# A pair's scores moved forward, to stand behind the transposes of the last pair but one

## The chip, the cores and the metric

The kernel runs on one core of a Trainium2 chip. The core has a matmul engine (TensorE, in the profile PE, with its weight loads as PEld), three engines for elementwise work (VectorE = DVE, ScalarE = ACT, GpSimd = POOL), and SyncE (SP), which here issues most DMAs. PE writes to a small accumulation memory, PSUM, and the other engines carry the sums from there to the main on-chip memory, SBUF. Each engine works through its own list of instructions in a fixed order; between engines, semaphores hold an instruction back until what it reads has been written and what it overwrites has been read.

The metric is the device time of one execution in microseconds (us), the median of several runs. Lower is better.

## What is computed

One decoder layer over 256 tokens and 1024 features in float32: a token mixer (a convolution module beside a sparse attention with three branches), a cross-attention to 256 memory tokens, and a gated feed-forward. The change is inside the sparse attention, in its branches "slc" (selected blocks) and "win" (window). With 256 tokens the four blocks of 64 are all selected and the window of 512 holds all, so that both branches come to causal softmax attention of 16 heads over all earlier keys, each with keys and values of its own. Cut to that:

```python
def masked_softmax(s, mask):
    s = jnp.where(mask, s, -1e30)
    m = jnp.max(s, axis=-1, keepdims=True)
    p = jnp.where(mask, jnp.exp(s - m), 0.0)
    return p / jnp.maximum(jnp.sum(p, axis=-1, keepdims=True), 1e-30)

def win_block(args):                      # slc: the same with ks, vs
    ...
    bias = rel_bias[t5_bucket(dist)]...
    s = jnp.einsum("bqgrd,bkgd->bgrqk", qb, kb) * scale + bias
    p = masked_softmax(s, mask)
    return jnp.einsum("bgrqk,bkgd->bqgrd", p, vb)
...
o = g[:, :, 0] * o_cmp + g[:, :, 1] * o_slc + g[:, :, 2] * o_win
```

The other large matmuls that matter here are projections of the token mixer (`g_conv`, in the kernel "gc") and of the cross-attention's values ("v").

## The kernel before

**Heads in pairs.** The 16 heads are worked on as eight pairs, hp = 0 to 7. `scores(hp)` (L738) does the matmuls of queries with keys for both branches at once. The queries come as two blocks of 128. The second block sees all 256 keys, so its *wide* scores are 128x512 (two branches of 256 keys), into one PSUM tile `s1_<head>` per head (tag "s", two buffers). The first block sees only the first 128 keys, so its *narrow* scores are 128x256 per head, and both heads share one PSUM tile `s0_<hp>` (tag "s0", one buffer). Each score is two matmuls, one with the high and one with the low part of the keys (`kdh`, `kdl`). DVE then adds the bias tile `nb<hp>` and takes the row minimum (the queries are negated) in one instruction: L754 for the wide ones, into `p1_<head>`, L759 for the narrow ones, into `p0_<hp>`. In the trace the tile names lose their numbers, so s0 and s1 are both "s" and p0 and p1 are both "p": the line and the shape tell them apart.

**The steps of a pair.** `weights(hp)` (L764) lets ACT take the eight exponentials (L769 wide, L773 narrow), and DVE the sums' reciprocals and the scaling. `turned` (L789) transposes p on PE: eight transposes of 128x128 into two tiles pt_a, and four into one tile pt_b. After each tile an ACT copy (L797) brings it to SBUF as ptt_a, ptt_b. pt_a has PSUM buffers of its own (tag "pt", two); **pt_b has the one buffer of tag "s0"**, the same that the narrow scores use. `outputs` (L800) multiplies the transposed p with the values, once for every two pairs, and DVE multiplies that into the gate tile `sga` (L820).

**What runs between.** To keep PE busy, `between()` (L825) hands out the projections gc0 to gc3 and v0 to v3 in *rows*: `rest(n)` does the next n of them. A chunk of weights is two halves (gc1_0, gc1_1), each split by ACT into a high part (L184, "gc1_0h") and by DVE into a low part (L186, "gc1_0l"). A row is eight matmuls of 128x256, and a half has three rows: high weights twice, low weights once. The raw halves lie in four buffers, the high and the low parts in five each.

**The order.** The loop at L872 goes through the pairs. Its body, for pair hp: `scores(hp + 1)` and (from hp = 1 on) `weights(hp + 1)`; some rows of the projections; the transposes of pair hp; two or three more rows; behind every second pair, `outputs`. `in_line()` and `last` chain the matmuls of PE in the order written; `behind(...)` puts an instruction behind a marked one. The framework then fixes one list per engine ahead of the run. So what stands in a list is known, and what waits there is seen only in a run. Three LayerNorm steps of the convolution are woven in at hp = 2 (sum, mean `mu`, squares), 4 and 5.

Of the kernel before, what the change touches and what calls it, by code (L numbers as in the profile page):

```python
# [15 lines left out]
P = 128  # L16
# [81 lines left out]
def tile_hybrid_block(  # L98
# [16 lines left out]
    nc = tc.nc  # L115
# [39 lines left out]
    def aux(name, shape, tag, bufs):  # L155
        return axp.tile(shape, F32, tag=tag, name=name, bufs=bufs)
# [35 lines left out]
    first, splits, paused = {}, {}, []  # L192
    aside = CHUNKS[CHUNK_AT["u1"]:CHUNK_AT["gc0"]]

    def behind(*marks):

        stack = ExitStack()
        for m in marks:
            stack.enter_context(tc.issue_after(m.ins))
        return stack  # L200
# [38 lines left out]
    last = []  # L239

    def in_line():
        return behind(*last)
# [155 lines left out]
    for i in range(4):  # L398
        hs = slice(2 * i, 2 * i + 2)
        for kb in (2 * i, 2 * i + 1):  # L400
            vec = nc.vector.scalar_tensor_tensor(out=hf[:, kb], in0=xt_t[:, kb], scalar=col(PP_GMIX, kb),
                                                 in1=r1, op0=ALU.mult, op1=ALU.mult)
# [62 lines left out]
    for j in range(NB):  # L465
# [3 lines left out]
        vec = nc.vector.tensor_tensor(out=vt[j][:, PAD:], in0=ps[:, 0], in1=sg, op=ALU.mult)  # L469
# [230 lines left out]
    def qh(hd, qb):  # L700
        return qt[hd // 8][:, hd % 8, qb * P:qb * P + P]
# [33 lines left out]
    def heads_of(hp):  # L735
        return 2 * hp, 2 * hp + 1

    def scores(hp):  # L738

        g = hp // 2  # L740
        nbp = bias_of(hp)
        s0 = aux(f"s0_{hp}", [P, 2, 2, P], "s0", 1)
        p0 = small(f"p0_{hp}", [P, 2, 2, P], tag="p0", bufs=2)
        p1 = []
        for k, hd in enumerate(heads_of(hp)):
            s1 = aux(f"s1_{hd}", [P, 2, S], "s", 2)
            with in_line():
                for i, t in enumerate((kdh, kdl)):
                    nc.tensor.matmul(s1, lhsT=qh(hd, 1), rhs=t[:, g].rearrange("p b t -> p (b t)"), start=i == 0, stop=i == 1)  # L749
                for i, t in enumerate((kdh, kdl)):  # L750
                    mm = nc.tensor.matmul(s0[:, k], lhsT=qh(hd, 0), rhs=t[:, g, :, 0:P], start=i == 0, stop=i == 1)
            p1.append(small(f"p1_{hd}", [P, 2, S], tag="pr", bufs=4))
            for br in range(2):
                nc.vector.tensor_tensor_reduce(out=p1[k][:, br], in0=s1[:, br], in1=nbp[:, k], scale=1.0, scalar=3e38,  # L754
                                               op0=ALU.add, op1=ALU.min, accum_out=mins[:, hd, 1, br:br + 1])
        last[:] = [mm]
        for k, hd in enumerate(heads_of(hp)):
            for br in range(2):
                least = nc.vector.tensor_tensor_reduce(out=p0[:, k, br], in0=s0[:, k, br], in1=nbp[:, k, P:S], scale=1.0, scalar=3e38,  # L759
                                               op0=ALU.add, op1=ALU.min, accum_out=mins[:, hd, 0, br:br + 1])  # L760
        first["scores"] = least,
        return p0, p1
# [82 lines left out]
    def rest(n):  # L845
        for _ in range(n):
            next(work)
# [22 lines left out]
    pct = [small(f"pct{c}", [P, 2, S], F32R, tag=t, bufs=n) for c, t, n in (("h", "vw", 4), ("l", "pctl", 1))]  # L870
    done = []
    for hp, n in enumerate((7, 7, 6, 6, 6, 6, 6, 4)):  # L872
        if hp < 7:
            with behind(*[vec] * (hp == 0)):
                p.append(scores(hp + 1))
            if hp == 0:
                first["gc1_0"] = first["scores"]
            if hp:
                weights(hp + 1, *p[hp + 1])

        late = 3 if 0 < hp < 7 else 2
        rest(n - late)
        with behind(*last):
            if hp == 2:
                with behind(*paused):
                    total = layer_norm_sum()
                layer_norm_centre(total)
            elif hp == 4:
                total = rnorm(total, "l")
            elif hp == 5:  # L890
                layer_norm_scale(total)
        if hp == 0:
            pc_ps = aux("pc_ps", [P, 4, P], "o", 1)
            with in_line():
                for qb in range(2):
                    for i in range(2):
                        mm = nc.tensor.transpose(pc_ps[:, 2 * i + qb], nsc[:, qb, 8 * i:8 * i + 8].rearrange("p h n -> p (h n)"), ident)
            last[:] = [mm]
            part(*[pct[c].rearrange("p i q -> p (i q)") for c in range(2)], pc_ps.rearrange("p i q -> p (i q)"))
        p0, p1 = p[hp]  # L900
        ta = [turned(f"a{hd}", [q for br in range(2) for q in (p0[:, k, br], p1[k][:, br, 0:P])])
              for k, hd in enumerate(heads_of(hp))]
        tb = turned(f"b{hp}", [p1[k][:, br, P:S] for k in range(2) for br in range(2)])
        if hp == 0:

            with behind(copies[-1]):
                first["gc3_0"] = weights(1, *p[1])[-1],
        if hp == 2:

            with behind(copies[-1]):  # L910
                total = layer_norm_squares()
        rest(late)
        done.append((hp, ta, tb))
        if hp % 2:
            outputs(done)
            done.clear()
# [574 lines left out]
```

## Time and profile before

| | |
|---|---|
| Time, median of 3 runs | 531.26 us (530.31 to 532.86) |
| The profiled execution's own time | 530.05 us |
| Its span in the profile | 528.0 us |
| Instructions of PE / DVE / ACT / POOL | 4315 / 871 / 599 / 110 |
| The eight pairs' scores, first and last start | 148.7 and 226.5 us |
| Longest waits of PE in the whole run | 1.1 us at its first instruction, 0.3, 0.2 us |

The span runs from the first instruction to the last; the execution's own time is some 2 us longer. An engine's busy time is the sum over its instructions, overlaps counted once. Starts are in microseconds from the start of the span. Idle time of an engine that isn't the bottleneck costs nothing by itself. In the trace's rows, "x8" is a count of like instructions that follow each other, and a bracket behind a row is idle time of that engine just before it and what ended it.

### The profile page before, as it was taken

How to read it: one execution, taken by the hardware profiler on the slowest of the kernel's cores; microseconds unless marked ns; L12 is line 12 of the kernel's file. 1: busy time of each engine (PE TensorE's matmuls, PEld its weight loads, DVE VectorE, ACT ScalarE, POOL GpSimd, SP SyncE). 2: the span in 40 equal slices, each digit the busy share in tenths (PEclk: the TensorE clock that was granted, in tenths of full speed). 3: DMA queues.
4: the chain of work that ended last, by engine and by line, in shares of the span. 5: the costliest groups of instructions: out<-in, count | busy, mean ns of one | idle time of the engine just before them, and what ended most of it. 6: DMA issues, size and time to landing. Idle time of an engine off the chain costs nothing.

```text
span 528.0 us, 11119 instructions
## 1 busy us (share of the span) xinstructions
PE 520.4 (99%) x4315; PEld 503.0 (95%) x4315; DVE 433.4 (82%) x871; ACT 343.7 (65%) x599; POOL 156.1 (30%) x110
## 2 busy tenths in 40 slices
PE   9999999999999999999999999999999999999995
PEld 8999999999999999999999999999999999988884
DVE  4868899999978898975969676697989888878984
ACT  4676466787656988789447664575556655647553
POOL 0069999999971200300004000330000000000001
PEclk9999999999999999999999999999999999999999
DMA  8927964664355443347764643858755577455622
GB/s 316 418 91 263 352 189 161 201 219 160 121 180 181 166 154 128 112 147 213 233 208 166 234 161 108 239 173 274 215 197 193 200 242 226 157 137 171 226 81 81
DMA packets 30740, 101.55 MB, mean 192 GB/s; under 512 B 3296, under 2 KB 5856, under 8 KB 30304
## 3 DMA queue, kind: packets, MB, share of 16 engines
q1 hardware_dynamic: 29104, 96.99, 54.1%
q0 software_dynamic: 864, 2.62, 3.0%
q10 hardware_dynamic: 720, 1.23, 0.6%
q8 instruction: 34, 0.56, 0.4%
q14 instruction: 18, 0.15, 0.1%
HBM read 99.59 MB, written 1.25 MB: 191 GB/s over the span
## 4 chain that ended last, share of the span: by engine, by line
PE 60%; DVE 1%; ACT 0%; issue 0%; ACTq 0%; DVEq 0%
PE ps_f L255 23%; PE fo L1247 6%; PE ps_v L255 4%; PE ps_pw L255 4%; PE ps_xo L255 4%; PE ps_wo L255 4%; PE ps_xq L255 4%; PE m L1247 4%; PE xs L985 1%; PE xo_ps L985 1%; PE o L815 1%; PE pt_a L794 1%; PE s L749 1%; PE o L812 1%; PE pt_b L794 0%; PE o L806 0%
## 5 line engine op out<-in xcount | busy, mean ns | idle before, releaser
L433 DVE SCALAR_TENSOR_TENSOR yp<-vt,ppt,yp 128x256 f32<-128x256 f32 x204 | 81.7, 485 | 0.2
L255 PE MATMUL ps_f<-g,f_1h 128*128 128x256 f32 x352 | 44.2, 277 | 0.0
L255 PE MATMUL ps_f<-g,f_0h 128*128 128x256 f32 x352 | 43.6, 276 | 0.0
L255 PEld LDWEIGHTS ps_f<-g,f_1h 128*128 128x128 f32 x352 | 41.8, 188 | 0.1
L255 PEld LDWEIGHTS ps_f<-g,f_0h 128*128 128x128 f32 x352 | 41.5, 188 | 0.0
L184 ACT ACTIVATE f_0h<-f 128x1024 fp32r<-128x1024 f32 x22 | 23.3, 1057 | 14.8 <-issue 6.7
L186 DVE TENSOR_TENSOR f_1l<-f,f_1h 128x1024 fp32r<-128x1024 f32 x22 | 27.5, 1249 | 6.4 <-ACT f_1h L184 5.5
L184 ACT ACTIVATE f_1h<-f 128x1024 fp32r<-128x1024 f32 x22 | 23.3, 1061 | 13.6 <-PE ps_f L255 10.1
L186 DVE TENSOR_TENSOR f_0l<-f,f_0h 128x1024 fp32r<-128x1024 f32 x22 | 26.7, 1213 | 1.6 <-ACT f_0h L184 1.6
L186 POOL TENSOR_TENSOR u_0l<-u,u_0h 128x1024 fp32r<-128x1024 f32 x7 | 17.4, 2486 | 30.2 <-PE ps_k L255 30.2
L255 PE MATMUL ps_f<-g,f_0l 128*128 128x256 f32 x176 | 23.8, 276 | 0.0
L255 PE MATMUL ps_f<-g,f_1l 128*128 128x256 f32 x176 | 23.5, 276 | 0.0
L255 PEld LDWEIGHTS ps_f<-g,f_0l 128*128 128x128 f32 x176 | 21.7, 188 | 0.0
L255 PEld LDWEIGHTS ps_f<-g,f_1l 128*128 128x128 f32 x176 | 21.6, 188 | 0.0
L769 ACT ACTIVATE p<-p,mins 128x256 f32<-128x256 f32 x32 | 15.9, 503 | 8.2 <-DVE mins L754 8.2
L1213 DVE TENSOR_TENSOR ab<-ps_f,r 128x512 f32<-128x512 f32 x22 | 15.1, 689 | 7.4 <-PE ps_f L255 7.4
L1134 POOL DMA_DIRECT2D spare<-in_wfo_dram x1 | 0.9, 866 | 64.3 <-DVE uh L300 64.3
L186 POOL TENSOR_TENSOR u_1l<-u,u_1h 128x1024 fp32r<-128x1024 f32 x7 | 18.0, 2572 | 0.0
L445 POOL TENSOR_TENSOR yt<-yt,vw 128x512 f32<-128x512 f32 x13 | 17.1, 1313 | 0.0
L1215 ACT ACTIVATE sl<-ab 128x256 f32<-128x256 f32 x22 | 9.2, 419 | 11.2 <-DVE ab L1213 11.2
L255 PE MATMUL ps_u<-hh,u_0h 128*128 128x256 f32 x128 | 16.1, 276 | 0.0
L1289 POOL TENSOR_TENSOR x<-y,gf 128x512 f32<-128x512 f32 x2 | 2.6, 1308 | 45.3 <-issue 45.2
(612 smaller groups left out, 1630.4 us busy)
## 6 DMA issues: line engine op xcount, KB each, us to landing
f<-in_wst_dram SPq DMA_DIRECT2D x44, 512.0 KB, 4.1
fo<-in_wfo_dram SPq DMA_DIRECT2D x16, 512.0 KB, 3.2
u<-in_wst_dram SPq DMA_DIRECT2D x14, 512.0 KB, 8.2
q<-in_wst_dram SPq DMA_DIRECT2D x8, 512.0 KB, 4.2
ga<-in_wst_dram SPq DMA_DIRECT2D x8, 512.0 KB, 3.7
gc<-in_wst_dram SPq DMA_DIRECT2D x8, 512.0 KB, 3.9
v<-in_wst_dram SPq DMA_DIRECT2D x8, 512.0 KB, 5.8
pw<-in_wst_dram SPq DMA_DIRECT2D x8, 512.0 KB, 4.8
```

The lines of the kernel that those rows point to most:

```text
L184: copy = nc.scalar.activation(hi, w, AF.Copy)
L186: splits[name] = copy, eng.tensor_tensor(out=lo, in0=w, in1=f(hi[:]), op=ALU.subtract)
L255: mm = nc.tensor.matmul(ps[:, b], lhsT=lhsT, rhs=rhs, start=row + b + kb == 0, stop=kb == NB - 1 and row == 2 and b == 1)
L433: nc.vector.scalar_tensor_tensor(out=out[:, i] if t == ts[-1] else acc[i], in0=v, scalar=w, in1=acc[i], op0=ALU.mult, op1=ALU.add)
L445: nc.gpsimd.tensor_tensor(out=yt[:, 0:2], in0=yt[:, 0:2], in1=pr, op=ALU.add)
L749: nc.tensor.matmul(s1, lhsT=qh(hd, 1), rhs=t[:, g].rearrange("p b t -> p (b t)"), start=i == 0, stop=i == 1)
L769: exp.append(nc.scalar.activation(p1[k][:, br], p1[k][:, br], AF.Exp, scale=-1.0, bias=mins[:, hd, 1, br:br + 1], accum_out=sums[:, hd, 1, ...
L794: mm = nc.tensor.transpose(ps[:, i], src, ident)
L985: mm = nc.tensor.matmul(o, lhsT=lhsT, rhs=rhs, start=n == 0, stop=n == len(order) - 1)
L1213: scaled[:] = [nc.vector.tensor_tensor(out=ab, in0=ps, in1=rf.unsqueeze(1).to_broadcast([P, 2, S]), op=ALU.mult)]
L1215: silu = nc.scalar.activation(sl, ab[:, 0], AF.Silu)
L1247: mm = nc.tensor.matmul(o, lhsT=a[x], rhs=b[w], start=start and n == 0, stop=stop and n == 2)
```

## The change

`scores` is cut in two. First come the wide scores of both heads, with their minima; then a function that is handed in (`between`); then the narrow scores of both heads, which before stood behind each head's wide ones, and whose s0 buffer is now asked for only there. In the loop, `scores(hp + 2)` is called directly behind the transposes of pair hp, for hp = 0 to 5, with one row of the projections between its wide and its narrow part; before, it was called at the start of the next turn of the loop, that is, behind the two or three rows and the outputs that close pair hp. `weights` stays at the start of the turn. The counts of all rows, scores and transposes are as before.

```diff
-    def scores(hp):
+    def scores(hp, between=lambda: None):
...
-        s0 = aux(f"s0_{hp}", [P, 2, 2, P], "s0", 1)
         p0 = small(f"p0_{hp}", [P, 2, 2, P], tag="p0", bufs=2)
         p1 = []
         for k, hd in enumerate(heads_of(hp)):
             s1 = aux(f"s1_{hd}", [P, 2, S], "s", 2)
             with in_line():
                 for i, t in enumerate((kdh, kdl)):
-                    nc.tensor.matmul(s1, lhsT=qh(hd, 1), rhs=t[:, g].rearrange("p b t -> p (b t)"), start=i == 0, stop=i == 1)
-                for i, t in enumerate((kdh, kdl)):
-                    mm = nc.tensor.matmul(s0[:, k], lhsT=qh(hd, 0), rhs=t[:, g, :, 0:P], start=i == 0, stop=i == 1)
+                    mm = nc.tensor.matmul(s1, lhsT=qh(hd, 1), rhs=t[:, g].rearrange("p b t -> p (b t)"), start=i == 0, stop=i == 1)
...
+        last[:] = [mm]
+        between()
+        s0 = aux(f"s0_{hp}", [P, 2, 2, P], "s0", 1)
+        with in_line():
+            for k, hd in enumerate(heads_of(hp)):
+                for i, t in enumerate((kdh, kdl)):
+                    mm = nc.tensor.matmul(s0[:, k], lhsT=qh(hd, 0), rhs=t[:, g, :, 0:P], start=i == 0, stop=i == 1)
         last[:] = [mm]
...
     for hp, n in enumerate((7, 7, 6, 6, 6, 6, 6, 4)):
-        if hp < 7:
-            with behind(*[vec] * (hp == 0)):
-                p.append(scores(hp + 1))
-            if hp == 0:
-                first["gc1_0"] = first["scores"]
-            if hp:
-                weights(hp + 1, *p[hp + 1])
+        if hp == 0:
+            with behind(vec):
+                p.append(scores(1))
+            first["gc1_0"] = first["scores"]
+        elif hp < 7:
+            weights(hp + 1, *p[hp + 1])
...
-        rest(late)
+        if hp < 6:
+            p.append(scores(hp + 2, lambda: rest(1)))
+        rest(late - (hp < 6))
         done.append((hp, ta, tb))
         if hp % 2:
             outputs(done)
```

How the lists of the engines move. In them a tile has its full name: `s1_6` and `s1_7` are the wide scores of pair 3, `s0_3` its narrow ones, `pt_b1` the transposes of pair 1 that lie in the s0 buffer.

PE before, behind the transposes of pair 1; the rest of the outputs `o_0` follows, and only then the scores of pair 3:

```order
L794 MATMUL pt_b1_2509<-cpt_67,p1_2_2276 128x128 x2
L794 MATMUL pt_b1_2509<-cpt_67,p1_3_2284 128x128 x2
L255 MATMUL ps_gc1_2399<-hh_84,gc1_1l_2476 128x256 x8
L255 MATMUL ps_gc2_2525<-hh_84,gc2_0h_2528 128x256 x16
L806 MATMUL o_0_2548<-pcth_2264,vcm_1174 128x256
```

PE after the change, at the same place:

```order
L798 MATMUL pt_b1_2509<-cpt_67,p1_2_2273 128x128 x2
L798 MATMUL pt_b1_2509<-cpt_67,p1_3_2279 128x128 x2
L748 MATMUL s1_6_2520<-kdh_1536,qt_1175 128x512
L748 MATMUL s1_6_2520<-kdl_1537,qt_1175 128x512
L748 MATMUL s1_7_2526<-kdh_1536,qt_1175 128x512
L748 MATMUL s1_7_2526<-kdl_1537,qt_1175 128x512
L255 MATMUL ps_gc1_2424<-hh_84,gc1_1l_2476 128x256 x8
L759 MATMUL s0_3_2541<-kdh_1536,qt_1175 128x256
L759 MATMUL s0_3_2541<-kdl_1537,qt_1175 128x256
L759 MATMUL s0_3_2541<-kdh_1536,qt_1175 128x256
L759 MATMUL s0_3_2541<-kdl_1537,qt_1175 128x256
L255 MATMUL ps_gc2_2550<-hh_84,gc2_0h_2553 128x256 x16
```

The eight score matmuls of pair 3 have come forward past two rows of gc2 and the outputs; one row of gc1 stands between its wide and its narrow part.

ACT before, from the end of pair 1's exponentials to the copy of `pt_b1` (`p1_4`, `p1_5`, `p0_2` are the exponentials of pair 2; `sgc` is the copy of a gate projection):

```order
L773 ACTIVATE p0_1_2270,sums_1973<-p0_1_2270,mins_1975 128x128 x4
L838 ACTIVATE sgc_1905<-ps_gc0_2291 128x512
L184 ACTIVATE gc3_0h_2702<-gc3_0_2700 128x1024
L769 ACTIVATE p1_4_2424,sums_1973<-p1_4_2424,mins_1975 128x256 x2
L769 ACTIVATE p1_5_2432,sums_1973<-p1_5_2432,mins_1975 128x256 x2
L773 ACTIVATE p0_2_2418,sums_1973<-p0_2_2418,mins_1975 128x128 x4
L184 ACTIVATE gc3_1h_2775<-gc3_1_2773 128x1024
L797 ACTIVATE ptt_a2_2500<-pt_a2_2495 128x512
L184 ACTIVATE v0_0h_2828<-v0_0_2826 128x1024
L797 ACTIVATE ptt_a3_2507<-pt_a3_2502 128x512
L797 ACTIVATE ptt_b1_2514<-pt_b1_2509 128x512
```

ACT after the change, the same stretch:

```order
L777 ACTIVATE p0_1_2269,sums_1973<-p0_1_2269,mins_1975 128x128 x4
L773 ACTIVATE p1_4_2397,sums_1973<-p1_4_2397,mins_1975 128x256
L842 ACTIVATE sgc_1905<-ps_gc0_2291 128x512
L773 ACTIVATE p1_4_2397,sums_1973<-p1_4_2397,mins_1975 128x256
L773 ACTIVATE p1_5_2403,sums_1973<-p1_5_2403,mins_1975 128x256 x2
L777 ACTIVATE p0_2_2393,sums_1973<-p0_2_2393,mins_1975 128x128 x4
L184 ACTIVATE gc3_0h_2727<-gc3_0_2725 128x1024
L184 ACTIVATE gc3_1h_2775<-gc3_1_2773 128x1024
L184 ACTIVATE v0_0h_2853<-v0_0_2851 128x1024
L801 ACTIVATE ptt_a2_2500<-pt_a2_2495 128x512
L801 ACTIVATE ptt_a3_2507<-pt_a3_2502 128x512
L801 ACTIVATE ptt_b1_2514<-pt_b1_2509 128x512
```

Between the two ends stand the same instructions; the exponentials of pair 2 have come forward past a split, and the three copies now stand together at the end.

ACT before, at the copies of pair 3 (`p1_9` and `p0_4` are exponentials of pair 4):

```order
L184 ACTIVATE v2_0h_3140<-v2_0_3138 128x1024
L769 ACTIVATE p1_9_2740,sums_1973<-p1_9_2740,mins_1975 128x256
L797 ACTIVATE ptt_a6_2800<-pt_a6_2795 128x512
L769 ACTIVATE p1_9_2740,sums_1973<-p1_9_2740,mins_1975 128x256
L773 ACTIVATE p0_4_2726,sums_1973<-p0_4_2726,mins_1975 128x128 x4
L797 ACTIVATE ptt_b3_2814<-pt_b3_2809 128x512
```

And after the change:

```order
L773 ACTIVATE p1_9_2703,sums_1973<-p1_9_2703,mins_1975 128x256 x2
L184 ACTIVATE v1_1h_3077<-v1_1_3075 128x1024
L777 ACTIVATE p0_4_2693,sums_1973<-p0_4_2693,mins_1975 128x128 x4
L663 ACTIVATE sq2_6_2686<-yt_353 128x512
L184 ACTIVATE v2_0h_3165<-v2_0_3163 128x1024
L801 ACTIVATE ptt_b3_2814<-pt_b3_2809 128x512
L801 ACTIVATE ptt_a6_2800<-pt_a6_2795 128x512
```

Here the exponentials of pair 4 have moved ahead of the copies, and the copy of `pt_b3` stands first among them.

## The prediction

> **What bounds the kernel now.** I read the page first, then the stretches of time around the attention stage, then TensorE's (PE) and ScalarE's (ACT) instructions in order of time.
>
> ```profile
> PE 520.4 (99%) x4315; PEld 503.0 (95%) x4315; DVE 433.4 (82%) x871; ACT 343.7 (65%) x599; POOL 156.1 (30%) x110
> ```
>
> PE is busy 520.4 of 528.0 us. In the stretches view the columns are busy time and count of each engine, then the granted clock, the DMA share and GB/s:
>
> ```profile
> 169.00:183.00 14.00, 14.00 (x128) 13.41 (x128) 10.98 (x41) 14.00 (x45) 4.76 (x5) 1.00 0.53 186
> 180.00:200.00 20.00, 19.82 (x172) 18.21 (x171) 18.82 (x63) 17.34 (x46) 0.00 (x0) 1.00 0.42 137
> ```
>
> So PE streams through the stage, and lost 0.18 us of these 20. Whatever wait is taken away there, PE can gain little; whatever wait is added to PE is paid in full, because nothing behind it has slack to give. The first row says a second thing: from 169 to 183 us ACT too is busy 14.00 of 14.00 us. It is no bound of the whole, but in this stretch it works off a backlog without a gap.
>
> Now PE itself. A row is start, time, engine, line, operation, out<-in, count. A matmul's time overlaps the next one's, so what one costs is the distance between starts.
>
> ```profile
> 148.72 0.48 PE L749 MATMUL s<-kdh,qt 128*128 128x512 f32 x1
> 149.04 0.39 PE L749 MATMUL s<-kdl,qt 128*128 128x512 f32 x1
> ...
> 169.26 0.60 PE L794 MATMUL pt_b<-cpt,p 128*128 128x128 f32 x4
> ...
> 170.62 1.07 PE L255 MATMUL ps_gc<-hh,gc_0h 128*128 128x256 f32 x8
> 171.53 0.39 PE L749 MATMUL s<-kdh,qt 128*128 128x512 f32 x1
> ...
> 172.46 0.28 PE L751 MATMUL s<-kdh,qt 128*128 128x256 f32 x1
> ...
> 172.91 1.07 PE L255 MATMUL ps_gc<-hh,gc_0h 128*128 128x256 f32 x8
> ...
> 176.55 1.03 PE L794 MATMUL pt_a<-cpt,p 128*128 128x128 f32 x8
> 177.42 0.60 PE L794 MATMUL pt_b<-cpt,p 128*128 128x128 f32 x4
> 177.78 1.18 PE L255 MATMUL ps_gc<-hh,gc_1l 128*128 128x256 f32 x8
> ...
> 189.65 0.60 PE L794 MATMUL pt_b<-cpt,p 128*128 128x128 f32 x4
> ...
> 196.93 1.03 PE L794 MATMUL pt_a<-cpt,p 128*128 128x128 f32 x8
> 198.14 0.63 PE L794 MATMUL pt_b<-cpt,p 128*128 128x128 f32 x4 [0.18 <-DVE mins L759]
> ...
> 219.06 0.60 PE L794 MATMUL pt_b<-cpt,p 128*128 128x128 f32 x4
> ```
>
> From these: a row of eight matmuls costs 171.53 - 170.62 = 0.91 us; four wide scores 172.46 - 171.53 = 0.93; four narrow ones 172.91 - 172.46 = 0.45; a pair's eight pt_a transposes 177.42 - 176.55 = 0.87 and its four pt_b 177.78 - 177.42 = 0.36. The first wide score behind fp32 matmuls (the transposes are such) takes 149.04 - 148.72 = 0.32 instead of 0.23, so four wide scores right behind the transposes cost 0.93 + 0.09 = 1.02 us. The bracket at 198.14 is the stage's only PE wait: pt_b of pair 3 waits until VectorE (DVE) has read pair 4's narrow scores, because both live in the one buffer of tag s0.
>
> ACT's rows, among them the copies (L797) that empty pt_b:
>
> ```profile
> 170.04 0.62 ACT L797 ACTIVATE ptt_b<-pt_b 128x512 f32<-128x512 f32 x1
> ...
> 174.03 0.59 ACT L838 ACTIVATE sgc<-ps_gc 128x512 f32<-128x512 f32 x1
> 174.51 1.06 ACT L184 ACTIVATE gc_0h<-gc 128x1024 fp32r<-128x1024 f32 x1
> 175.46 0.51 ACT L769 ACTIVATE p<-p,mins 128x256 f32<-128x256 f32 x1
> ...
> 178.97 1.06 ACT L184 ACTIVATE gc_1h<-gc 128x1024 fp32r<-128x1024 f32 x1
> 179.92 0.59 ACT L797 ACTIVATE ptt_a<-pt_a 128x512 f32<-128x512 f32 x1
> 180.39 1.07 ACT L184 ACTIVATE v_0h<-v 128x1024 fp32r<-128x1024 f32 x1
> 181.35 0.59 ACT L797 ACTIVATE ptt_a<-pt_a 128x512 f32<-128x512 f32 x1
> 181.82 0.60 ACT L797 ACTIVATE ptt_b<-pt_b 128x512 f32<-128x512 f32 x1
> ...
> 190.79 0.59 ACT L797 ACTIVATE ptt_b<-pt_b 128x512 f32<-128x512 f32 x1
> 191.27 0.63 ACT L660 ACTIVATE ssum<-yt 128x512 f32<-128x512 f32 x1
> ...
> 192.83 0.59 ACT L838 ACTIVATE sgc<-ps_gc 128x512 f32<-128x512 f32 x1
> ...
> 201.09 0.58 ACT L797 ACTIVATE ptt_b<-pt_b 128x512 f32<-128x512 f32 x1
> ...
> 220.46 0.59 ACT L797 ACTIVATE ptt_b<-pt_b 128x512 f32<-128x512 f32 x1
> ```
>
> The reader should see how late a copy lands after the last transpose ended: pair 0, 170.66 - 169.86 = 0.80 us; pair 1, 182.42 - 178.02 = **4.40**; pair 2, 191.38 - 190.25 = 1.13; pair 3, 201.67 - 198.77 = 2.90; pair 5, 221.05 - 219.66 = 1.39. Before the change nobody needs the copy soon: the next user of s0 comes half a period later or behind the outputs.
>
> **The change part by part.** *Work on PE.* It has the same matmuls in another order, at 0. Whatever stood behind the fp32 transposes paid the 0.09 of the turn before as well. I leave ±0.1 for the LayerNorm mean's fp32 matmuls, which now split pair 4's wide scores.
>
> *The new wait.* In the changed order PE does, behind pt_b of pair hp: four wide scores (1.02), one row of eight (0.91), then the narrow scores of pair hp + 2, which write the s0 buffer that pt_b filled, and so wait for its copy. The cover is 1.02 + 0.91 = 1.93 us from the end of issue of pt_b; its last transpose ends 0.24 later (178.02 against 177.78), so 1.69 us are left for the copy. Against the lags above: pair 0, 0.80, no wait; pair 1, 4.40 - 1.69 = **2.71**; pair 2, 1.13, none with 0.5 to spare; pair 5, 1.39, none with 0.3; pair 3, 2.90 - 1.69 = 1.21, if its lag stays. Queued behind the waiting narrow scores on PE is everything: the gate rows, the outputs, and with them DVE and ACT.
>
> *Does pair 1's lag stay?* The work of ACT between the last exponential of pair 1 (174.03) and this copy is, in the two orders, the same set: one gate copy, two gc3 splits, one v0 split, eight exponentials of pair 2, three copies. Only their sequence changes, with all three copies now last. Before, this set ran from 174.03 to 182.42 without a gap, so earlier inputs cannot shorten it, and the exponentials' inputs come no later than before, since pair 2's scores are moved forward. The copy of pt_b lands at 182.42 again. PE gets to the narrow scores at 177.78 + 1.93 = 179.71. It waits 2.71 us, and a little more for the release, which this DVE row shows:
>
> ```profile
> 197.91 0.09 DVE L759 DVE_READ_ACCUMULATOR2_ANT mins<- 128x1 f32 x1
> ```
>
> It ended at 198.00, and the waiting pt_b started at 198.14. I take 0.1: **+2.8 us**.
>
> *Does pair 3's lag stay?* Before, the second half of pair 4's exponentials stood ahead of that copy, so ACT was late; now all eight stand earlier, and the copy of pt_b goes first of the three. Counted from the copy of pair 2: eight exponentials 178.97 - 175.46 = 3.51, four squares of (192.83 - 191.27) / 3 = 0.52, a gate copy 0.48, two splits of 0.95 (179.92 - 178.97), the copy 0.60: 8.6 us, so it lands 1.13 + 8.6 = 9.7 us after the end of pair 2's transposes. PE needs from there 1.02 + 0.91 + 0.45 + 5 x 0.91 + 0.87 + 0.36 + 1.02 + 0.91 - 0.24 = 9.85 us. They meet. I take no wait, and keep 0 to 1.2 us.
>
> *Wait removed.* pt_b of pair 3 waited for pair 4's minima: starts 198.14 - 196.93 = 1.21 apart instead of 0.87. Between pair 4's narrow scores and that pt_b PE now does five rows and eight transposes (5 x 0.91 + 0.87 = 5.4 us), before it was three and eight (3.6). The minima have 1.8 us more, where 0.34 were missing: **-0.34 us**. Late next would be the minima again, behind DVE's subtractions for the LayerNorm; they would need to lose those 1.8.
>
> *Other engines and queues.* No DMA, no POOL or SP instruction changes place; the bias loads wait for narrow minima that come 1 us earlier or at most with PE's shift later, and every weight load is behind the same splits. Moving the exponentials forward gives ACT slack that only PE could turn into time, and PE has none to get: 0.
>
> [...]
>
> **Sum:** +2.8 + 0 - 0.34 = **+2.45 us**. Against the profiled execution's 530.05 us that is 532.5. This execution lies 1.2 us below the median of the runs shown, 531.26; the same difference on the median gives **533.7 us**, which I forecast (+0.46%).
>
> **The rivals.** *A. The wait doesn't come.* Then only -0.34 is left: 530.9, faster by a hair. It needs pair 1's copy to land by 179.7, 2.7 us sooner, or PE to reach that point as much later. For it: ACT's times in that stretch could vary from run to run. Against it: no gap, the same set, the copies at the set's end.
>
> *B. A second wait.* Pair 3's copy stands behind squares and exponentials which wait on DVE; DVE does four subtractions for the LayerNorm between pair 4's minima. If that costs ACT a microsecond, pair 3's copy misses PE by up to the 1.2 us bound: 533.7 + 1.2 = 534.9. It decides from 0.1 us of ACT's waiting on. The 0.5 and 0.3 to spare of the copies of pairs 2 and 5 could go too; against that, they ran so before.
>
> *C. The clock falls in the wait.* The last rows of the stretches view:
>
> ```profile
> 520.00:523.00 3.00, 2.14 (x19) 1.94 (x17) 2.86 (x9) 2.01 (x6) 0.00 (x0) 1.00 0.04 15
> 523.00:526.00 3.00, 0.00 (x0) 0.00 (x0) 1.22 (x5) 0.88 (x2) 0.00 (x0) 1.00 0.69 265
> 526.00:528.00 2.00, 0.00 (x0) 0.00 (x0) 0.00 (x0) 0.00 (x0) 0.00 (x0) 0.62 0.28 104
> ```
>
> PE stops at 522.14, and the granted clock is still 1.00 up to 526: it fell after 3.86 us of idling at the earliest. A wait of 2.8 us is shorter. Should it fall all the same, at 0.62 for as long as a fall takes here, 3.86 us, that is 3.86 x (1 / 0.62 - 1) = 2.4 us: 536.1. [...]
>
> **How the numbers follow.** The forecast, one wait of 2.3 to 3.2 us, 0.62, with its own range of 532.9 to 534.4 (531.26 - 0.34 + the wait, and 0.3 for the median); rival A 0.13; B 0.19; C 0.04; what I didn't think of 0.02. The median itself moves by about half a microsecond in three runs (530.31 to 532.86). The range that leaves out 2 in 10 reaches from rival A's 530.9 to beyond B: 530.9 to 535.6. A measurement of this kernel tells about 0.5% (2.7 us) from no change, which puts the border at 533.9, inside my forecast: slower takes 0.38 of the forecast's 0.62, and B and C, 0.46; faster needs a gain that no row shows, 0.04; within 0.5% is left 0.50.
>
> **What would show it.** Right: on PE one new wait of 2.5 to 3 us on ACT's ptt_b copy, at the narrow scores of pair 3 near 179.7 us; no wait left at pt_b of pair 3; PE's busy share down by that wait, all later stages shifted by about 2.5 us and otherwise alike; ACT without a gap from 169 to 182.4. Wrong: no wait there (A), a second one at the narrow scores of pair 5, or of 4 or 7 (B), a granted clock below 1.00 behind the wait (C), or a time gained in a stage behind the attention, which I say has nothing to gain.

## The result, and the profile after

| | before | after |
|---|---|---|
| Median, executions timed side by side | 532.15 us (6 executions) | **541.53 us** (6 executions) |
| Lowest and highest | 530.31, 536.99 | 536.80, 542.47 |
| The profiled execution's own time | 530.05 us | 541.56 us |
| Its span | 528.0 us | 539.5 us |

The ratio of the times on record is 1.013, with a 95% interval of 1.0087 to 1.0174: the change made the kernel slower. Forecast were 533.7 us, at most 535.6. The six executions after the change stand in two groups, 536.8 and 537.1, and 541.5 to 542.5; those before do as well, only with more of them in the lower group (four of six). So one median comes from a lower group and the other from an upper one, and they lie 1.8% apart. That gap will matter.

The span is 11.5 us longer. Cut at four places, each a row of PE in both traces, nearly all of it is lost in three stretches. (Behind the attention PE does the projections named pw, wo, xq, xo and f in the traces, in this order: pw and wo end the token mixer, xq and xo belong to the cross-attention, f to the feed-forward.)

| Stretch | before | after | more |
|---|---|---|---|
| start to pair 0's pt_b | 169.26 | 169.36 | 0.1 |
| to pair 7's pt_b | 67.60 | 72.12 | **4.5** |
| to the first xq row | 44.08 | 45.89 | **1.8** |
| to the first feed-forward row (f) | 62.95 | 63.56 | 0.6 |
| to the end of the span | 184.1 | 188.6 | **4.5** |

**The stretch from pair 0's to pair 7's pt_b** holds the forecast wait. PE after the change, in order of time (start, time, engine, line, operation):

```profile
178.88 1.08 PE L255 MATMUL ps_gc<-hh,gc_1l 128*128 128x256 f32 x8
182.56 0.49 PE L759 MATMUL s<-kdh,qt 128*128 128x256 f32 x1 [2.60 <-ACT ptt_b L801]
...
183.49 3.22 PE L255 MATMUL ps_gc<-hh,gc_0h 128*128 128x256 f32 x16
...
201.72 1.03 PE L798 MATMUL pt_a<-cpt,p 128*128 128x128 f32 x8
202.59 0.60 PE L798 MATMUL pt_b<-cpt,p 128*128 128x128 f32 x4
```

The row of eight started at 178.88, so the narrow scores of pair 3 could have started 0.91 later, at 179.79; they start at 182.56. The wait cost 2.77 us, and the bracket names ACT's copy. pt_b of pair 3 now stands 0.87 behind its pt_a, without the bracket of before. No other wait on ACT is in PE's list. The copy, among ACT's rows:

```profile
180.01 1.06 ACT L184 ACTIVATE v_0h<-v 128x1024 fp32r<-128x1024 f32 x1
180.95 1.07 ACT L801 ACTIVATE ptt_a<-pt_a 128x512 f32<-128x512 f32 x2
181.91 0.60 ACT L801 ACTIVATE ptt_b<-pt_b 128x512 f32<-128x512 f32 x1
```

It ends at 182.51, behind three splits and two other copies.

But 16 matmuls behind the wait take 3.22 us, against 1.98 elsewhere. The stretches view says why (length, then busy time and count of PE, PEld, DVE, ACT, POOL, then granted clock, DMA share, GB/s):

```profile
179.80:182.60 2.80, 0.20 (x3) 0.04 (x1) 2.80 (x12) 2.80 (x6) 0.00 (x0) 1.00 0.00 0
182.70:186.10 3.40, 3.40 (x17) 3.40 (x18) 3.40 (x10) 2.25 (x9) 0.00 (x0) 0.50 0.59 190
186.10:190.00 3.90, 3.90 (x43) 3.03 (x42) 0.64 (x5) 2.60 (x9) 0.00 (x0) 1.00 0.79 266
250.00:280.00 30.00, 30.00 (x257) 30.00 (x256) 20.49 (x24) 16.23 (x20) 0.00 (x0) 1.00 0.66 211
390.00:420.00 30.00, 30.00 (x257) 30.00 (x256) 25.78 (x43) 17.43 (x27) 0.00 (x0) 1.00 0.57 193
```

For 3.4 us behind the wait (182.69 to 186.10 in the trace's clock record) the granted clock is 0.50: half of that time, some 1.7 us, is lost once more (an estimate; below it comes out as 1.5 to 1.7). **The clock fell behind a wait of 2.6 us**, which the prediction gave a chance of 0.04.

**The later stretches** show in the last two of these rows. In 30 us PE got through 257 matmuls, at a granted clock of 1.00, busy all the time. The same two stretches before:

```profile
250.00:280.00 30.00, 30.00 (x267) 30.00 (x266) 24.00 (x29) 15.92 (x20) 1.45 (x2) 1.00 0.65 208
390.00:420.00 30.00, 30.00 (x267) 30.00 (x266) 26.71 (x44) 18.43 (x28) 0.00 (x0) 1.00 0.58 192
```

267 against 257. PE was "busy 30.00 of 30.00" both times, so busy time cannot show this; only the count in a fixed stretch, or the distance of starts, can. A row of 16 is (1.98 - 0.28) / 15 = **113 ns** from start to start in one trace, (2.05 - 0.28) / 15 = **118 ns** in the other (0.28 is a single matmul's time). The two spacings are steady: in both traces no stream of 54 or more matmuls changes from one to the other before other matmuls come in between. The 912 matmuls behind the transposes fo keep 113.3 ns from 363 to 466 us before and 117.8 ns from 370 to 477 us after (means of 24 in a row, from the seventh on).

**What stands ahead of the slow stream.** PE before, from the last pair's pt_b over the last outputs (L815) to the first xq row:

```profile
236.86 0.60 PE L794 MATMUL pt_b<-cpt,p 128*128 128x128 f32 x4
...
242.21 0.60 PE L815 MATMUL o<-ptt_a,vst 128*64 128x256 f32 x4
242.74 2.10 PE L255 MATMUL ps_pw<-z,pw_0h 128*128 128x256 f32 x16
...
251.02 1.98 PE L255 MATMUL ps_pw<-z,pw_1h 128*128 128x256 f32 x16
...
280.94 0.39 PE L255 MATMUL ps_xq<-gh,xq_0h 128*128 128x256 f32 x2
```

And after the change:

```profile
241.48 0.60 PE L798 MATMUL pt_b<-cpt,p 128*128 128x128 f32 x4
...
245.53 0.60 PE L819 MATMUL o<-ptt_a,vst 128*64 128x256 f32 x4
246.06 1.19 PE L255 MATMUL ps_pw<-z,pw_0h 128*128 128x256 f32 x8
247.18 0.44 PE L816 MATMUL o<-ptt_b,vst 128*64 128x128 f32 x4
...
248.10 0.60 PE L819 MATMUL o<-ptt_a,vst 128*64 128x256 f32 x4
248.63 1.21 PE L255 MATMUL ps_pw<-z,pw_0h 128*128 128x256 f32 x8
...
250.62 2.05 PE L255 MATMUL ps_pw<-z,pw_1h 128*128 128x256 f32 x16
...
287.37 0.40 PE L255 MATMUL ps_xq<-gh,xq_0h 128*128 128x256 f32 x2
```

PE's list differs here too, 50 us behind the last moved score: the first eight pw matmuls now stand between the outputs of pairs 6 and 7. Nothing in the diff speaks of pw. Those rows are chained to nothing (the list `in_order` ends ahead of pw), so the framework is free to place them; why it chose another place after the change was not traced. From the second piece on the stream runs at 118 ns.

From the first xq row to the end PE's list is the same in both. The stretch from the first f row to the end, 184.1 against 188.6, differs by spacing alone, and by the same 4.5 us that separate the two groups of executions, after and before.

### The profile page after: what moved, and what is told of

It reads as the page before. It is cut to its first block, busy times and chain, and to the rows that moved or that the text cites. A ratio compares the mean times of both kernels' runs of the same rounds, so it can differ in the third digit from the quotient of the medians.

```text
span 539.5 us, 11118 instructions
## 1 busy us (share of the span) xinstructions
PE 529.8 (98%) x4315; PEld 512.1 (95%) x4315; DVE 433.9 (80%) x871; ACT 344.4 (64%) x599; POOL 155.5 (29%) x110
## 4 chain that ended last, share of the span: by engine, by line
PE 65%; DVE 1%; ACT 0%; issue 0%; DVEq 0%; ACTq 0%
PE ps_f L255 23%; PE fo L1252 6%; PE ps_pw L255 4%; PE ps_v L255 4%; PE ps_xq L255 4%; PE ps_wo L255 4%; PE ps_xo L255 4%; PE m L1252 4%; PE ps_gc L255 2%; PE o L819 1%; PE xs L990 1%; PE xo_ps L990 1%; PE pt_a L798 1%; PE o L816 1%; PE s L748 1%; PE s L759 1%
## 5 line engine op out<-in xcount | busy, mean ns | idle before, releaser
L255 PE MATMUL ps_f<-g,f_1h 128*128 128x256 f32 x352 | 45.7, 281 | 0.0
L255 PE MATMUL ps_f<-g,f_0h 128*128 128x256 f32 x352 | 45.0, 281 | 0.0
L255 PEld LDWEIGHTS ps_f<-g,f_1h 128*128 128x128 f32 x352 | 43.3, 189 | 0.1
L255 PEld LDWEIGHTS ps_f<-g,f_0h 128*128 128x128 f32 x352 | 42.9, 189 | 0.0
L1220 ACT ACTIVATE sl<-ab 128x256 f32<-128x256 f32 x22 | 9.2, 417 | 11.5 <-DVE ab L1218 11.4
L255 PE MATMUL ps_u<-hh,u_1h 128*128 128x256 f32 x128 | 16.0, 276 | 0.0
```

What stands on the lines that cost most here:

```text
L255: mm = nc.tensor.matmul(ps[:, b], lhsT=lhsT, rhs=rhs, start=row + b + kb == 0, stop=kb == NB - 1 and row == 2 and b == 1)
L1220: silu = nc.scalar.activation(sl, ab[:, 0], AF.Silu)
```

## The experiments

Theory at this point: the 11.5 us are the wait (2.8, less 0.3 for the one removed), the fallen clock (some 1.6), and runs of slow spacing for nearly all of the rest. Open were: does the clock's fall go with the wait, and from what length; is the slow spacing an after-effect of wait or clock, or of the order of PE's list, or mere chance?

### The wait made shorter, in three steps

Splits of ACT were put behind pair 1's copies, so that those land sooner: all three splits (shown), the last two, or the last one.

```diff
+        if hp == 1:
+            for name in ('gc3_0', 'gc3_1', 'v0_0'):
+                first[name] = copies[-1],
         if hp < 6:
             p.append(scores(hp + 2, lambda: rest(1)))
```

Three splits behind the copy:

> The changed kernel, with ACT's three splits gc3_0, gc3_1 and v0_0 put behind the copy of pt_b of pair 1. Theory: the new PE wait at pair 3's narrow scores is ACT's late copy, the half clock behind it follows from that wait, so both go: copy lands near 179.5 us, PE wait under 0.2 us, granted clock 1.00 from 180 to 190, transposes of pair 2 some 4.5 us earlier than in the changed kernel; about 530 us where the feed-forward streams at 113 ns a matmul, about 534.6 where it streams at 118 ns. Rival 1 (the slow stream is a lasting effect of the wait and the clock's fall): all runs near 530 and feed-forward at 113 ns. Rival 2 (the slow stream is drawn anew in each run, whatever happened in the attention): two groups of runs 4 to 5 us apart here too. Rival 3 (the lost time comes from the moved scores themselves, not from the wait): PE wait gone but still above 535.

Two:

> The splits gc3_1 and v0_0 put behind the copy: PE wait about 0.7 us. No fall of the clock expected under either idea of it: 530.5 us in the fast stream, 535 in the slow one. If a wait of any length changes the stream for good, the slow group only.

One:

> Only the split v0_0 put behind the copy: the copy lands 0.95 us sooner, so the PE wait shrinks from 2.6 to about 1.7 us. If any idle of a microsecond or two drops the clock: granted clock about 0.56 for 3.5 us behind it, another 1.7 us lost, 533.2 us in the fast stream. If the clock needs a longer idle: clock 1.00 and 531.5 us in the fast stream. With the slow stream 4.6 us more in both.

Measured: waits of 0.5, 0.7 and 1.7 us, and pair 0's to pair 7's pt_b in 68.47, 68.73 and 69.68 us. Before, it is 67.60. With two splits or one behind, the wait stands at the narrow scores of pair 3, as in the changed kernel. With three behind it is gone there, as expected, but another came, at pair 5's narrow scores, on the copy of pair 3:

```profile
201.15 0.38 PE L759 MATMUL s<-kdh,qt 128*128 128x256 f32 x1 [0.47 <-ACT ptt_b L801]
```

That is the place of the prediction's rival B. The copy stands second of the three on ACT here, where it stood first in the changed kernel.

Each excess over 67.60 is the wait and some 0.4 us; with the full wait of 2.6 it is 4.5, that is 1.9 more than the wait. So the clock's price comes only with the long wait. Where the wait is 1.7, with the stretches chosen 3.41 us long (the length of the fall above) and the first of them around the whole wait:

```profile
178.62:182.04 3.42, 1.77 (x13) 1.44 (x12) 3.23 (x18) 3.42 (x6) 0.00 (x0) 1.00 0.00 0
182.04:185.45 3.41, 3.41 (x32) 3.27 (x34) 3.41 (x13) 3.41 (x11) 0.00 (x0) 1.00 0.32 97
```

PE idled through 1.65 of 3.42 us, and the clock stayed.

The times as a whole came out above what had been expected (530 to 531.5 and 534.6 to 536.1): for three, two and one splits behind, medians of 537.85, 537.47 and 539.10 us against 535.45 of the kernel before, ratios of 1.005 (1.0019 to 1.0081), 1.0051 (1.0014 to 1.0088) and 1.007 (1.0034 to 1.0105). With hardly a wait and no fall some 2 us were still left. And the kernel before itself had here a median of 535.45, in two groups: nine of 35 executions between 529.5 and 532.3, none from there to 534.4, 26 above.

### Only the wide scores early

```diff
         last[:] = [mm]
-        between()
+        yield p0, p1
         s0 = aux(f"s0_{hp}", [P, 2, 2, P], "s0", 1)
...
         elif hp < 7:
+            next(narrow)
             weights(hp + 1, *p[hp + 1])
...
-            p.append(scores(hp + 2, lambda: rest(1)))
-        rest(late - (hp < 6))
+            narrow = scores(hp + 2)
+            p.append(next(narrow))
+        rest(late)
```

> Only one part of the change: the wide scores stand directly behind the transposes of the last pair but one, the narrow ones stay at the start of the next turn of the loop, behind the remaining rows and the outputs. Theory: no narrow score asks for the s0 buffer early, so no PE wait on the copy, clock 1.00: about 530 us in the fast stream (534.6 in the slow one). If the early wide scores themselves cost time: above 532 in the fast stream.

No wait was left, and no fall: 67.97 us from pair 0's to pair 7's pt_b. Yet the median was 537.51, ratio 1.0054 (1.0016 to 1.0092). Two executions lie at 532.3 and 532.8 and ten at 536.8 and above, 2 to 4 us over what had been expected for two groups (530 and 534.6), and the pw stage was slow all the same:

```profile
250.00:280.00 30.00, 30.00 (x257) 30.00 (x256) 20.51 (x23) 15.22 (x19) 0.00 (x0) 1.00 0.59 192
```

So the slow spacing there is no after-effect of the wait or of the clock. All four kernels tried so far have the first eight pw matmuls between the outputs, as the changed kernel has, and in all four 45.9 us lie between pair 7's pt_b and the first xq row.

### The kernel before once more

> The kernel before, unchanged, profiled a second time. Theory D (the spacing of PE's 128x256 rows is taken anew at each break in the stream, and then kept): its pw and wo rows, which follow the unsplit outputs, run at 113.4 ns again, so that 44.1 us lie between the last pair's pt_b and the first xq row, as in the first profile; its feed-forward rows run at 113.4 or 117.8 ns, and the time of the execution goes with that: 530 to 532 us with the first, 534.5 to 537 with the second. Theory W (the slow spacing is an after-effect of the new wait or of the fallen clock): no row of this kernel runs at 117.8 ns in the pw, wo and feed-forward stages, whatever its time.

537.07 us. The pw stage was fast again, 44.08 us to the first xq row. The feed-forward was not: 188.5 us to the end. In the first profile of this kernel the f rows ahead of the transposes fo (L1098) and behind them are

```profile
358.23 1.98 PE L255 MATMUL ps_f<-g,f_1h 128*128 128x256 f32 x16
...
360.96 1.91 PE L1098 MATMUL fo<-cpt,x 128*128 128x128 f32 x16
362.62 2.07 PE L255 MATMUL ps_f<-g,f_0h 128*128 128x256 f32 x16
...
365.44 1.98 PE L255 MATMUL ps_f<-g,f_1h 128*128 128x256 f32 x16
```

and in the second

```profile
355.40 2.05 PE L255 MATMUL ps_f<-g,f_1h 128*128 128x256 f32 x16
...
363.88 1.91 PE L1098 MATMUL fo<-cpt,x 128*128 128x128 f32 x16
365.55 2.13 PE L255 MATMUL ps_f<-g,f_0h 128*128 128x256 f32 x16
368.46 2.05 PE L255 MATMUL ps_f<-g,f_1h 128*128 128x256 f32 x16
```

One program, one list, two spacings: 1.98 and 2.05 for the same row of 16. This is the gap of 4.5 us between the groups, and it is not the change's. The stretch from the first xq row to the first f row, too, took 62.95 us in the one profile and 63.90 in the other.

### The pw rows chained behind the outputs

```diff
-    in_order = CHUNKS[CHUNK_AT["kc"]:CHUNK_AT["pw0"]]
+    in_order = CHUNKS[CHUNK_AT["kc"]:CHUNK_AT["pw0"] + 4]
```

In the changed kernel:

> The changed kernel with the pw rows chained behind the outputs, so that no pw row stands between the outputs of pairs 6 and 7. The wait of 2.6 us at pair 3's narrow scores stays, the clock falls behind it as before. Theory D: the pw and wo rows go back to 113.4 ns; from the last pair's pt_b to the first xq row 44.1 us instead of 45.9; fast executions near 535, slow ones near 539.5 us, some 2 us under the changed kernel's 537 and 541.5. Theory W: 45.9 us there, and 537 and 541.5 us as the changed kernel.

With the three splits behind pair 1's copy as well:

> The same, with the three splits behind pair 1's copy as well (wait 0.5 us, no fall of the clock). Theory D: 44.1 us from the last pair's pt_b to the first xq row; about 1 us over the kernel before at equal feed-forward spacing, so groups near 531.5 and 536, and the ratio within 0.3% of 1. Theory W: without wait and fall everything is at 113.4 ns, the feed-forward too, so that nearly all executions lie near 531.5.

In the changed kernel with this edit:

```profile
241.93 0.60 PE L798 MATMUL pt_b<-cpt,p 128*128 128x128 f32 x4
...
250.65 1.98 PE L255 MATMUL ps_pw<-z,pw_1h 128*128 128x256 f32 x16
...
286.01 0.39 PE L255 MATMUL ps_xq<-gh,xq_0h 128*128 128x256 f32 x2
```

44.08 us, as before the change, in both kernels; the wait of 2.60 us and the fall stayed in the first. Its executions lie at 535.2 (one) and at 539.7 to 541.2 (five), ratio 1.0106 (1.0047 to 1.0165): 1.0 to 1.7 us under the changed kernel's groups, where 2 had been expected. The second has no wait on ACT, no fall and no slow pw rows: 534.64 us against 535.09 for the kernel before beside it, ratio 1.001 (0.9966 to 1.0054), in groups of 531.4 to 533.4 and 535.9 to 538.3. Group against group it stands 0.3 us over the kernel before beside it (531.7 and 536.3 against 531.4 and 536.1, medians). **With wait, fall and split seam gone, the loss is gone to within 0.3 us.** That the feed-forward would be fast too, as the theory of an after-effect had it, did not come: six of its twelve executions are in the upper group.

The fall of the clock stood elsewhere here:

```profile
183.05 0.38 PE L759 MATMUL s<-kdh,qt 128*128 128x256 f32 x1 [2.60 <-ACT ptt_b L801]
...
183.63 2.89 PE L255 MATMUL ps_gc<-hh,gc_0h 128*128 128x256 f32 x16
```

```profile
181.03:184.44 3.41, 1.39 (x12) 1.39 (x13) 3.41 (x9) 3.41 (x11) 0.00 (x0) 1.00 0.00 0
184.44:187.85 3.41, 3.41 (x19) 3.19 (x19) 2.28 (x10) 2.25 (x6) 0.00 (x0) 0.50 0.86 276
```

The wait ended at 183.05, the scores behind it ran at full speed (from the second on 0.12 us from start to start, against 0.21 or 0.22 in the changed kernel), and the clock fell only 1.4 us later, at 184.44, while PE was at work. In the changed kernel it fell 0.1 us behind a wait of the same 2.60 us. So the fall doesn't come at a set time after the wait. In the 3.41 us ahead of the fall PE had idled for 2.02 us here and for 2.60 (76%) in the changed kernel; 1.65 of 3.42 us, in the kernel with one split behind, had no fall after it.

The clock's records of the two profiles before and after tell where the falls stand. They begin at 1.00, 4.23 and 5.19 us into the span. From there to the fall are 522.239 us before (the fall behind the program's end) and 177.493 us after; from the end of that fall to the next, behind the program's end, 351.573 us. The fall within the span lasts 3.413 us, and the three distances are 153, 52 and 103 times 3.4133 us. In these two traces the falls thus stand on steps of that length, which the wait did not start. What decides at a step was not shown beyond the idle times above.

### The break in the feed-forward moved

In the kernel before, the 16 fo transposes were put behind twelve more chunks.

```diff
-        if j == 2:
+        if j == 14:
             accs = residual_first()
```

> The kernel before with the 16 transposes of the second residual, which break the feed-forward stream at 361 us, moved behind twelve more chunks (to about 426 us). Theory D: the rows from 361 to 426 us keep the spacing of those ahead of them (113.4 ns in five of six profiles so far) and a new draw comes only at 426; a slow draw then costs 1.8 us instead of 4.5, so that most executions lie between 530 and 534 and the median is 2 us below the kernel before's 535.4. A rival F (the feed-forward's spacing is set by what the other engines and the DMAs do there, not by the break): the rows turn slow near 361 us as before in most executions, and the median stays at 535.4.

```profile
353.39 2.05 PE L255 MATMUL ps_f<-g,f_1h 128*128 128x256 f32 x16
...
429.71 1.91 PE L1098 MATMUL fo<-cpt,x 128*128 128x128 f32 x16
431.38 2.08 PE L255 MATMUL ps_f<-g,f_0h 128*128 128x256 f32 x16
...
434.20 1.98 PE L255 MATMUL ps_f<-g,f_1h 128*128 128x256 f32 x16
```

The rows kept one spacing for 78 us and changed it at the break, where the break now was: slow ahead of it, fast behind. That part of theory D held. Its bet on the first draw didn't: the rows ahead were slow, and the median of 535.02 us is that of the kernel before (ratio 1.0018, 0.9976 to 1.0060). But the two groups were gone from the twelve executions: they lie at 532.5 to 533.9, 534.9 to 535.2, 536.5 and above, three of them where the kernel before has none (532.9 to 534.4), as two draws of some 2 to 3 us each would make it. With one profile and twelve times that is a fit, not a proof.

### A longer wait

The row of eight between wide and narrow scores was put behind both.

```diff
-            p.append(scores(hp + 2, lambda: rest(1)))
-        rest(late - (hp < 6))
+            p.append(scores(hp + 2))
+        rest(late)
```

> The changed kernel without the row of eight between the wide and the narrow scores (that row stands behind them instead), so that the cover of the copy shrinks by 0.91 us. By the account so far: the wait at pair 3's narrow scores grows from 2.6 to 3.5 us; one window of 3.41 us at half clock follows again, costing 1.6 us as before and not more, since the fall is for one window whatever the wait; waits of 0.3 to 0.6 us come at the narrow scores of pairs 4 and 7, whose copies had 0.5 and 0.3 us to spare; the stage's end lies 1 to 2 us behind the changed kernel's; executions near 538 and 542.5 us. Rival: the fall grows with the wait (a second window at half clock), 1.6 us more again.

```profile
182.20 0.38 PE L759 MATMUL s<-kdh,qt 128*128 128x256 f32 x1 [3.33 <-ACT ptt_b L801]
```

```profile
179.30:182.72 3.42, 0.52 (x4) 0.52 (x5) 3.42 (x13) 3.42 (x8) 0.00 (x0) 1.00 0.00 0
182.72:186.13 3.41, 3.41 (x18) 3.41 (x18) 3.40 (x12) 3.27 (x15) 0.00 (x0) 0.50 0.56 192
186.13:189.50 3.37, 3.37 (x36) 2.95 (x36) 2.13 (x9) 1.32 (x2) 0.00 (x0) 1.00 0.79 215
```

The wait grew to 3.3 us, PE idled through 2.90 of the 3.42 us ahead of the fall, and the fall stayed 3.41 us long. Two more waits came, 0.5 and 0.2 us, at the narrow scores of pairs 5 and 7 (4 and 7 had been named). Pair 0's to pair 7's pt_b took 74.73 us, 2.6 more than in the changed kernel, where 1 to 2 had been expected; the waits account for 1.4 of it, and the rest was not followed up. The four executions lie at 543.4 to 546.1, over the 538 and 542.5 expected; median 545.14, ratio 1.0194 (1.0150 to 1.0238).

### Wide scores early, and the pw rows chained

> Only the wide scores moved forward, the narrow ones at the start of the next turn, and the pw rows chained behind the outputs: no wait, no fall, and the pw and wo rows at 113.4 ns. By the account so far nothing of the 6 us is left: groups near 530.5 and 535 us, as the kernel before, ratio within 0.3% of 1. If the earlier wide scores cost PE something by themselves (theory C), the groups lie 1 us or more above those of the kernel before.

No wait, no fall, 67.81 us from pt_b to pt_b and 44.07 to the first xq row, as before the change to 0.2 us. Its median was 535.82, ratio 1.0025 (0.9999 to 1.0050), and the lower group near 530.5 stayed empty: all twelve executions lie between 535.1 and 537.7, where the kernel before has its upper group (534.4 and up). So the wide scores cost 0.2 us in the stages that they touch (0.4 in the kernel without the chained rows), and yet this version is no better. Its profile has the slow feed-forward, 188.5 us; that the other eleven executions had it too is read from their times alone.

### All in one table

Each row is one profiled execution, in us; "wait on ACT" is the sum of PE's waits on copies of pt_b. Two stretches are left out, the start (169.0 to 172.2 us) and the one from the first xq to the first f row (63.0 to 64.0).

| Kernel | wait on ACT | pt_b to pt_b | to first xq row | f to end | own time |
|---|---|---|---|---|---|
| before | 0 | 67.60 | 44.08 | 184.1 | 530.05 |
| before, again | 0 | 67.59 | 44.08 | 188.5 | 537.07 |
| after | 2.6 | 72.12 | 45.89 | 188.6 | 541.56 |
| three splits behind | 0.5 | 68.47 | 45.89 | 188.5 | 538.42 |
| two splits behind | 0.7 | 68.73 | 45.89 | 184.1 | 533.60 |
| one split behind | 1.7 | 69.68 | 45.88 | 188.2 | 538.96 |
| wide only | 0 | 67.97 | 45.89 | 188.2 | 539.77 |
| after, pw chained | 2.6 | 72.09 | 44.08 | 188.5 | 540.48 |
| three splits, pw chained | 0 | 68.02 | 44.08 | 184.4 | 531.61 |
| fo late | 0 | 67.72 | 44.08 | 187.1 | 533.54 |
| no row between | 4.0 | 74.73 | 45.89 | 188.2 | 543.44 |
| wide only, pw chained | 0 | 67.81 | 44.07 | 188.5 | 537.67 |

The column "to first xq row" has two values to 0.01 us, and the order of PE's list at the seam alone tells which. The column "f to end" goes with no edit: from the first xq row on PE's list is the same in all of them but "fo late".

## Why the prediction was wrong

**Right.** The wait came where it was placed, at pair 3's narrow scores, on ACT's copy of pt_b of pair 1, at the size given (2.8 forecast, 2.77 measured); the copy landed at 182.51 (182.42 forecast). ACT worked without a gap up to it, 13.10 of 13.10 us from 169.4 to 182.5. Pair 3's wait for the minima went, and neither pair 5's nor any other wait on ACT came: rivals A and B did not happen. For B that was in part luck. The forecast had pair 3's copy and PE "meet" within 0.15 us; the copy landed at 204.22, 0.67 ahead of pair 5's narrow scores at 204.89, and in the kernel with three splits moved, without the long wait ahead of it, that wait did come (0.47 us). The gc_0h row queued behind the waiting scores did not pass them, as the forecast had it: it starts at 183.49, behind scores that start from 182.56 on.

**Wrong, step one: the bound on the clock** (rival C). "PE stops at 522.14, and the granted clock is still 1.00 up to 526: it fell after 3.86 us of idling at the earliest" is true of the kernel's end, but it was taken for how long PE must idle. It measures something else. The last row of the view there, 0.62 over 526 to 528, puts the fall at about 526.5 (0.48 us at 1.00 and the rest at 0.50 make 0.62; the clock's record has 526.46). In the 3.41 us ahead of it PE was idle throughout; one step of 3.41 us earlier, at 523.05, PE had been idle for 0.9 of 3.41 us, and no fall came. So the 3.86 us ran from the moment at which PE stopped, while the fall came on a step. How long PE must idle is not to be read from it: 2.60 us of idling in the 3.41 ahead of the fall at 182.69 were enough, and 2.02 in a later kernel. So C, which was given 0.04, came. Its price was wrong as well: 0.62 was the mean of a row that held both clocks, and 3.86 the idle time ahead of a fall, not a fall's length. C was priced at 2.4 us; measured, it is half clock for 3.41 us, and 72.12 - 67.60 is 4.5, less 2.6 for the wait and the 0.4 that the shorter waits carry as well, 1.5 to 1.7.

**Wrong, step two: "all later stages shifted by about 2.5 us and otherwise alike".** PE's "same matmuls in another order, at 0" was priced from the places where the scores moved. The list differs once more behind them, at the seam to pw, and a stream that starts there at 118 ns instead of 113 loses 1.8 us by the first xq row. Three pairs of kernels differ in that seam alone, and in each the chained one has 44.07 or 44.08 us there instead of 45.89. No row of the profile before showed the price, but that the list differed there could be seen beforehand.

**Wrong, step three: the median that all was added to.** 531.26 us was the median of three executions which all lay in the lower group, and the forecast let it move by half a microsecond. Over all 81 executions of the kernel before in this study 27 lie at 529.5 to 532.9, 54 at 534.4 and above, and none between; the median is 535.2. The changed kernel had four of six in its upper group. So of the measured 1.3%, part is how the draws fell. Group against group the change costs 536.9 - 531.0 = 5.9 us and 541.5 - 535.5 = 6.0 us (medians of the groups), 1.1%. The steps make 2.8 for the wait, -0.3 for the one removed, 1.6 for the clock and 1.8 at the seam, 5.9 in all. Inside the attention stage some 0.4 more go to the slow spacing again: of the 328 matmuls of the gc and v rows there 152 stand in streams at 118 ns after the change, 64 before. The 0.6 up to the feed-forward need no cause in the change, since the kernel before alone differs there by 0.95 from one profile to the other.

The forecast's 2.45 us was thus right for what it counted, and counted less than half. Of the 7.8 us between 533.7 and 541.5, 3.5 are what it did not count, and 4.3 come from a base in the lower group (531.26) where the measured median lay in the upper one (535.5 in the kernel before).

**Open.** What decides the spacing at a break isn't known: only that behind the transposes fo it was settled within the first six matmuls (starts 206, 116, 114, 113, 113 ns apart before, 201, 118, 118, 117, 118 after). For the seam the order decides, in twelve traces of twelve, but how it does so is not shown. For the feed-forward the order does not, since one program has both; but its odds seem to differ between programs (27 of 81 in the lower group before, none of 12 in the last kernel). What the clock does where PE idles for more than 1.65 and less than 2.02 of 3.41 us was not tried, nor whether a wait of 2.6 us can stand so that no fall follows.

## What to carry to other kernels

When an engine is busy to the last microsecond, price a new wait twice: once for its length, read from the lag of the copy it waits for, and once for the clock: here waits of 2.6 and 3.3 us were followed by 3.41 us at a granted clock of 0.50, and one of 1.65 us was not. Compare the engines' lists of the two kernels to their ends, not only where the edit is: a scheduler can move things far away from it. And look at single execution times before adding to a median: two groups with a gap mean that a few executions tell which group was drawn, not what the change did.

## What the runs showed of the hardware that was not expected

- The streams of 128x256 matmuls, each with its own weight load (352 and 352 in one group of the page), had two steady spacings at the same granted clock of 1.00: 113 and 118 ns (267 and 257 in 30 us). Behind the transposes fo, the profile before took the first and kept it for 103 us, the one after took the second and kept it for 107. PE is busy without a gap in both (30.00 of 30.00 us).
- The granted clock stood at 0.50 for 3.41 us after waits of 2.60 us (in two kernels) and of 3.33, and stayed at 1.00 after one of 1.65. PE had idled through 2.60, 2.02 and 2.90 of the 3.41 us ahead of the falls. They came 0.1, 1.4 and 0.5 us after the wait had ended, and in the two traces whose clock records were compared they stand a whole number of times 3.4133 us (52, 103, 153) from the record's begin or from the fall before.
